# How the first attention of a hybrid decoder layer turns the probabilities of two query blocks: by TensorE, or by transposing transfers

## The chip, the core and the metric

The kernel runs on one core of a Trainium2 chip. The metric is the device time of one execution in microseconds (us). A core has TensorE (PE, whose weight loads are shown as PEld), VectorE (DVE), ScalarE (ACT), GpSimd (POOL) and SyncE (SP, which here issues DMA transfers); each works through its own queue of instructions in order, and they meet through semaphores.

## The reference

The reference is one decoder layer on 1024 tokens behind 16 learned meta tokens, D = 1024, in fp32. One projection feeds two groups of heads; their outputs are joined, projected and added to the residual, and a SwiGLU block follows. Cut to what matters here:

```python
def hybrid_mixer(u, pos, topk, w_in, ...):
    ...
    o_mla = causal_block_attention(q_mla, k_mla, v_mla)              # 8 heads, dense and causal
    ...
    o_dsa = indexed_sparse_attention(q_s, k_s, v_s, q_i, k_i, w_i, topk)   # 8 heads, selected keys
    o = jnp.concatenate([o_mla.reshape(...), o_dsa.reshape(...)], axis=-1)
    return o @ w_o

# inside both attentions, for each block of 128 queries
s = jnp.einsum('bqhd,bkhd->bhqk', qb, k) * scale
s = jnp.where(mask, s, -jnp.inf)
p = jax.nn.softmax(s, axis=-1)
o = jnp.einsum('bhqk,bkhd->bqhd', p, v)

h = h + hybrid_mixer(rmsnorm(h, ...), ...)
h = h + swiglu(rmsnorm(h, ...), w_gate, w_up, w_down)
return rmsnorm(h, final_norm_g)[:, N_META:t]
```

## The kernel before, in words

Queries are cut into eight blocks of 128. Attention is done in two passes: the **first attention** takes query blocks 0, 1 and 2 (`BLK_A`), the **second** blocks 3 to 7 (`BLK_B`). Each runs over 16 heads, first the eight latent ones (`mla_head`, half 0), then the eight sparse ones (`dsa_head`, half 1). Between and around them lie the first out-projection, the feed-forward block of the first 384 rows, the second out-projection and the feed-forward block of the rest. The matrix products of the attention scores and the feed-forward block are each made of two or three passes over a high and a low part of their operands.

The work is written as Python generators that are interleaved by hand, and the framework's scheduler then sets the order of the instructions in each engine's queue by a timeline of its own; an instruction that is later in the program can so stand earlier in a queue, if it is ready by that timeline. During the first heads of the first attention the rest of the latent projections (`mla_rest`, for rows 384 and up) is interleaved, and the first 12 tiles of the output weights are split into a high and a low part on GpSimd (`wo_load`, lines 995 and 996). The feed-forward block of the first rows fills TensorE during the second attention.

In each head and query block `b`, `scores` makes the scores by TensorE, adds the mask and finds the row's extreme in VectorE (line 785), and takes the exponential on ScalarE (line 792). Key blocks are 128 wide and there are `b + 2` of them. What is left is to turn the probabilities round, keys onto partitions, as a high and a low fp16 part, for the value product in `values` (lines 823 to 825: three matmuls for each key block). There are two ways to do that.

Where `b` is in `by_pe`, TensorE transposes the fp32 probabilities (line 799), ScalarE casts them out of PSUM to the high part (line 801) and VectorE makes the low part (line 802), both into tile `pE`. Otherwise, with a constant added to the extreme (line 790), the high part is cast in place of the rows into a buffer `hl` (line 812, VectorE), GpSimd subtracts it in pieces to give the low part (line 814), and SyncE issues one transfer that transposes both into tile `pT` (line 816):

```python
for c in cuts(n, 264):
    G.tensor_sub(pl_[:, c], pb[:, c], ph[:, c])
pT = pl.tile([P, 2 * (cfg["b1"] + 2), P], F16, name="pT", bufs=cfg["pT"])
nc.sync.dma_start_transpose(pT[:, 0:2 * nt], hl[:, 0:2 * nt * P])
```

The value products lag behind: finished probabilities wait in the list `todo`, and a block's values are taken when `depth` entries are in it. In the tables `CFG_A` and `CFG_B`, `hl`, `pT`, `pE`, `pb`, `pd`, `q`, `v` and `kn` are numbers of buffers. SyncE's queue also carries the loads of each sparse head: its keys and queries into `dkn` (two buffers) and `dkm` (one buffer), lines 917 and 923, its values into `vh` (two buffers), line 875, and the tiles of the output weights `wor` (line 991).

Of the kernel before, what the change touches and what calls it, by code (L numbers as in the profile page):

```python
# [43 lines left out]
BLK_A, BLK_B = tuple(range(NA)), tuple(range(NA, NB))  # L44
# [17 lines left out]

PREP_AT, PREP_N, WO_AT = 6, 2, 150
PH_ACT = BLK_B, ()
CFG_A = dict(depth=3, by_pe=set(BLK_A), order=list(BLK_A), pd=2, hl=2, pT=2, pb=3, pE=3, q=2, v=2, kn=2, ahead=0)
CFG_B = dict(depth=4, by_pe=set(), order=list(BLK_B), pd=2, hl=2, pT=2, pb=2, pE=2, q=2, v=2, kn=2, ahead=3)


# [30 lines left out]
def hybrid_layer(ctx, tc, a, out):  # L99
# [1046 lines left out]

    cfg = dict(CFG_A, s=ps_s, t=ps_t, o=ps_o, ck=(ckH, ckL), wk=(wkH, wkL), sel=selb, kT=kT_a, q_rows=q_a, v_rows=v_a)
    woa = ExitStack()
# [104 lines left out]
```

## Time and profile before

| what | value |
|---|---|
| time, median of 3 runs | 1523.28 us (1520.2 to 1530.37) |
| profiled execution: its own time | 1528.41 us |
| profiled execution: span of the instructions | 1526.6 us |
| TensorE busy | 1434.4 us, 94% of the span |
| VectorE busy | 907.2 us, 59% |
| ScalarE busy | 846.6 us, 55% |
| GpSimd busy | 796.2 us, 52% |
| share of the chain that ended last | PE 29%, of which lines 189 to 191 some 10% each |

Shares over the whole span are means over stages that have different limits. The first attention is the stretch from some 346 to 441 us, the second from 485 to 955 us. Busy times of single stretches and single instructions stand in the rows below; times in those rows count from the start of the span.

### The profile page before, as it was taken

Reading aid. Unit: us, or ns where it says so; the run is one execution under the profiler, and the core shown is the slowest. Engines: PE = TensorE matmul, PEld = TensorE weight load, DVE = VectorE, ACT = ScalarE, POOL = GpSimd, SP = SyncE. Lnnn points to the kernel's source line nnn. Section 1 sums busy time; section 2 is a strip of 40 time slices with the busy share of each in tenths; the row PEclk is TensorE's granted clock in tenths of the full one; section 3 lists DMA queues with packets and bytes.
Section 4 is the critical chain, followed back from the end, with each engine's and each line's share of the span. In section 5 each row is a group of like instructions: output and inputs, shape, how many; then the busy total and the mean of one; then the engine's idle time right before and its main releaser. Section 6 shows DMA issues by size and latency. Waiting matters only on the chain. (4 is left out here: it accounts for less than half of the span.)

```text
span 1526.6 us, 29766 instructions
## 1 busy us (share of the span) xinstructions
PE 1434.4 (94%) x10584; PEld 1332.2 (87%) x10584; DVE 907.2 (59%) x2447; ACT 846.6 (55%) x2038; POOL 796.2 (52%) x1121
## 2 busy tenths in 40 slices
PE   6999998999989899899899999999999999999997
PEld 5999998888778788788798899888899999999996
DVE  6879989948886876966866666415422222213225
ACT  5666678797889889797544453435412122122223
POOL 2663555212405678786887888531634344343342
PEclk9999999999999799999999999999999999999999
DMA  6123355224434787587799997431322222222221
GB/s 180 50 52 85 86 136 125 47 88 143 125 103 107 163 187 171 138 182 148 177 212 200 204 210 172 138 108 39 125 82 84 67 85 65 74 83 70 83 70 69
DMA packets 353732, 180.71 MB, mean 118 GB/s; under 512 B 196560, under 2 KB 341344, under 8 KB 353584
## 3 DMA queue, kind: packets, MB, share of 16 engines
q1 hardware_dynamic: 353584, 178.82, 46.7%
q8 instruction: 83, 1.36, 0.4%
q14 instruction: 65, 0.53, 0.1%
HBM read 120.77 MB, written 21.30 MB: 93 GB/s over the span
## 5 line engine op out<-in xcount | busy, mean ns | idle before, releaser
L184 POOL TENSOR_TENSOR wL<-raw,wH 128x256 fp32r<-128x256 f32 x528 | 399.1, 787 | 303.0 <-ACT wH L181 293.3
L181 ACT ACTIVATE wH<-raw 128x1024 fp32r<-128x1024 f32 x132 | 139.7, 1058 | 263.2 <-PE b L191 96.4
L189 PE MATMUL b<-ub,wH 128*128 128x384 f32 (+1 forms) x704 | 218.6, 311 | 1.2 <-ACT wH L181 1.2
L190 PE MATMUL b<-ub,wH 128*128 128x384 f32 (+1 forms) x704 | 218.5, 311 | 0.0
L191 PE MATMUL b<-ub,wL 128*128 128x384 f32 (+1 forms) x704 | 217.8, 310 | 0.0
L814 POOL TENSOR_TENSOR hl<-pd,hl 128x260 f16<-128x260 f32 (+5 forms) x256 | 168.4, 686 | 72.6 <-ACT hl L810 39.6
L189 PE MATMUL b<-wh,uH 128*128 128x256 f32 (+3 forms) x568 | 169.1, 298 | 5.3 <-DVE mlo L311 2.6
L191 PE MATMUL b<-wh,uL 128*128 128x256 f32 (+3 forms) x568 | 168.5, 297 | 0.0
L190 PE MATMUL b<-wl,uH 128*128 128x256 f32 (+3 forms) x568 | 168.1, 296 | 0.1
L1107 DVE TENSOR_TENSOR oh<-b,oh 128x512 f32<-128x512 f32 x146 | 99.2, 686 | 74.5 <-PE b L191 74.1
L189 PE MATMUL b<-wH,hH 128*128 128x512 f32 x352 | 140.5, 399 | 1.8 <-DVE oh L1107 0.8
L190 PE MATMUL b<-wL,hH 128*128 128x512 f32 x352 | 138.7, 394 | 0.0
L191 PE MATMUL b<-wH,hL 128*128 128x512 f32 x352 | 136.0, 393 | 0.4 <-DVE hL L186 0.4
L189 PEld LDWEIGHTS b<-ub,wH 128*128 128x128 f32 x704 | 132.8, 189 | 3.1 <-ACT wH L181 1.5
L190 PEld LDWEIGHTS b<-ub,wH 128*128 128x128 f32 x704 | 132.2, 188 | 1.2
L191 PEld LDWEIGHTS b<-ub,wL 128*128 128x128 f32 x704 | 132.1, 188 | 1.1
L189 PE MATMUL b<-ua,wH 128*128 128x384 f32 x352 | 122.0, 347 | 4.0 <-ACT wH L181 4.0
L375 ACT ACTIVATE js<-sc,bs 128x528 bf16<-128x528 int16 (+7 forms) x128 | 120.8, 944 | 4.1 <-DVE sc L430 1.7
L191 PE MATMUL b<-ua,wL 128*128 128x384 f32 x352 | 121.0, 344 | 0.0
L190 PE MATMUL b<-ua,wH 128*128 128x384 f32 x352 | 120.9, 343 | 0.0
L1093 DVE SCALAR_TENSOR_TENSOR sg<-sg,b 128x384 f32<-128x384 f32 x66 | 33.5, 508 | 144.5 <-ACT sg L1092 144.5
L189 PEld LDWEIGHTS b<-wh,uH 128*128 128x128 f32 x568 | 108.6, 191 | 7.4 <-DVE mlo L311 3.4
(326 smaller groups left out, 4026.6 us busy)
## 6 DMA issues: line engine op xcount, KB each, us to landing
raw<-in_w_gate SPq DMA_DIRECT2D x44, 512.0 KB, 4.1
raw<-in_w_up SPq DMA_DIRECT2D x44, 512.0 KB, 4.0
raw<-in_w_down SPq DMA_DIRECT2D x44, 512.0 KB, 3.6
wor<-in_w_o SPq DMA_DIRECT2D x64, 128.0 KB, 2.6
wraw<-in_w_in SPq DMA_DIRECT2D x40, 128.0 KB, 2.3
vh<-v_x SPq DMA_DIRECT2D x16, 288.0 KB, 3.8
xt<-in_x SPq DMA_DIRECT2D x8, 512.0 KB, 4.3
ks_x<-st SPq DMA_DIRECT2D x32, 128.0 KB, 2.2
```

The source lines that it names most:

```text
L181: S.activation(h, src, AF.Copy)
L184: G.tensor_sub(l[:, c], src[:, c], h[:, c])
L189: PE.matmul(o, lh, rh, start=first, stop=False)
L190: PE.matmul(o, lh, rl, start=False, stop=False)
L191: PE.matmul(o, ll, rh, start=False, stop=last)
L375: S.activation(act_junk()[:, :n_keys(b)], y[b], AF.Sign, bias=cols[0], accum_out=cnt)
L814: G.tensor_sub(pl_[:, c], pb[:, c], ph[:, c])
L1093: V.scalar_tensor_tensor(sg, sg, 1.0, pg, op0=OP.add, op1=OP.mult)
L1107: V.tensor_add(oh[t][:, cs], po, oh[t][:, cs])
```

## The change

The table of the first attention is altered in one line. Only block 0 stays with TensorE; the probabilities of blocks 1 and 2 take the other way, cast, subtracted and transposed by a transfer. `todo` becomes one entry deeper, there are three `hl` buffers and four `pT`, and the buffers of TensorE's way go from three to two.

```diff
 PREP_AT, PREP_N, WO_AT = 6, 2, 150
 PH_ACT = BLK_B, ()
-CFG_A = dict(depth=3, by_pe=set(BLK_A), order=list(BLK_A), pd=2, hl=2, pT=2, pb=3, pE=3, q=2, v=2, kn=2, ahead=0)
+CFG_A = dict(depth=4, by_pe={0}, order=list(BLK_A), pd=2, hl=3, pT=4, pb=2, pE=2, q=2, v=2, kn=2, ahead=0)
 CFG_B = dict(depth=4, by_pe=set(), order=list(BLK_B), pd=2, hl=2, pT=2, pb=2, pE=2, q=2, v=2, kn=2, ahead=3)
```

Since the scheduler sets the order anew, instructions of other lines move as well. Three places follow; a row gives the line, the operation, the tiles (out<-in), the size, and how often it stands there in a row.

GpSimd's queue in the later latent heads of the first attention: the difference between before (-) and after (+). `wor`, `woh` and `wol` are a raw tile of the output weights and its two parts.

```order
+L814 TENSOR_TENSOR hl_5318<-pd,hl_5318 128x136 x2
+L814 TENSOR_TENSOR hl_5319<-pd,hl_5319 128x200 x2
+L995 TENSOR_SCALAR woh<-wor 128x256 x2
+L996 TENSOR_TENSOR wol<-wor,woh 128x256
+L814 TENSOR_TENSOR hl_5320<-pd,hl_5320 128x136 x2
+L995 TENSOR_SCALAR woh<-wor 128x256 x2
+L996 TENSOR_TENSOR wol<-wor,woh 128x256
+L814 TENSOR_TENSOR hl_5318<-pd,hl_5318 128x200 x2
 L995 TENSOR_SCALAR woh<-wor 128x256
-L996 TENSOR_TENSOR wol<-wor,woh 128x256 x3
-L995 TENSOR_SCALAR woh<-wor 128x256 x3
```

The splits of the output weights stood by themselves; now the subtractions of blocks 1 and 2 stand between them.

SyncE's queue in the sparse heads of the first attention, before:

```order
L923 DMA dkm<-ks_m 16x128
L917 DMA dkn<-ks_x 128x3x128
L917 DMA dkn<-qs_x 128x3x128
L875 DMA vh<-v_x_94 128x2x256
L923 DMA dkm<-ks_m 16x128
```

The same place after:

```order
L816 DMA_TRANSPOSE pT<-hl_5320 128x8x128
L816 DMA_TRANSPOSE pT<-hl_5318 128x6x128
L917 DMA dkn<-ks_x 128x3x128
L923 DMA dkm<-ks_m 16x128
L875 DMA vh<-v_x_94 128x2x256
L917 DMA dkn<-qs_x 128x3x128
L816 DMA_TRANSPOSE pT<-hl_5319 128x8x128
L816 DMA_TRANSPOSE pT<-hl_5320 128x6x128
```

Two transposing transfers per head (six 128-column blocks for query block 1, eight for block 2) now stand in the one queue with the loads. The load of `vh` waits until the values that last used its buffer are done, as it did.

TensorE's queue where the second attention ends and the second out-projection begins, before. `ua`, `wH`, `hH` belong to the feed-forward block of the first rows, `oh` is the joined output of the heads, `ub` its transposed halves:

```order
L191 MATMUL b_15676<-ua,wL 128x384
L189 MATMUL b_15731<-wH,hH 128x512
L190 MATMUL b_15731<-wL,hH 128x512
L191 MATMUL b_15731<-wH,hL 128x512
L189 MATMUL b_15739<-wH,hH 128x512
L190 MATMUL b_15739<-wL,hH 128x512
L191 MATMUL b_15739<-wH,hL 128x512
L189 MATMUL b_12518<-woh,ub 128x256
```

The same place after:

```order
L825 MATMUL b_12347<-vh,pT 128x64
L1014 MATMUL b_12399<-ident,oh_5124 128x128 x4
L1014 MATMUL b_12406<-ident,oh_5125 128x128 x4
L1014 MATMUL b_12413<-ident,oh_5125 128x128 x4
L189 MATMUL b_12512<-woh,ub 128x256
L189 MATMUL b_12542<-woh,ub 128x256
```

Matmuls of the feed-forward block stood between the last values and the first products of the out-projection; now the first products follow the transposes directly.

## Rows read from the trace of the kernel before

**Rows 1.** Busy time of each engine, by stretch of the first attention; granted clock, DMA share.

```profile
346.00:372.00 26.00, 24.71 (x161) 21.41 (x160) 22.68 (x65) 18.86 (x53) 7.22 (x16) 0.93 0.34 106
372.00:380.00 8.00, 7.38 (x82) 6.61 (x81) 6.33 (x20) 6.67 (x22) 1.75 (x4) 1.00 0.80 259
380.00:400.00 20.00, 19.55 (x229) 17.11 (x227) 16.71 (x52) 18.21 (x65) 17.64 (x24) 1.00 0.50 147
400.00:436.00 36.00, 30.99 (x363) 26.40 (x362) 30.85 (x93) 29.38 (x103) 0.64 (x1) 1.00 0.37 102
```

**Rows 2.** ScalarE's timeline: block 0's exponential of heads 3, 8 and 15.

```profile
379.45 0.42 ACT L792 ACTIVATE pb<-pb,sm 128x144 f32<-128x144 f32 x1 [0.27 <-DVE sm L785]
...
402.11 0.41 ACT L792 ACTIVATE pb<-pb,sm 128x144 f32<-128x144 f32 x1 [0.38 <-DVE sm L785]
...
435.73 0.41 ACT L792 ACTIVATE pb<-pb,sm 128x144 f32<-128x144 f32 x1
```

**Rows 3.** Groups by line and shape, 405 to 440 us.

```profile
L799 PE MATMUL b<-ident,pb 128*128 128x128 f32 x67 | 11.5, 282 | 1.8 <-DVE pE L802 0.9 <-ACT pb L792 0.8
...
L802 DVE SCALAR_TENSOR_TENSOR pE<-b,pE 128x512 f16<-128x512 f32 x8 | 5.5, 685 | 0.9 <-ACT pE L801 0.9
...
L802 DVE SCALAR_TENSOR_TENSOR pE<-b,pE 128x384 f16<-128x384 f32 x8 | 4.4, 553 | 0.6 <-ACT pE L801 0.6
...
L801 ACT ACTIVATE pE<-b 128x384 f16<-128x384 f32 x7 | 3.5, 498 | 1.0 <-PE b L799 1.0
```

**Rows 4.** TensorE's timeline within one sparse head.

```profile
411.28 0.64 PE L799 MATMUL b<-ident,pb 128*128 128x128 f32 x4
411.76 0.19 PE L825 MATMUL b<-vh,pE 128*128 128x64 f16 x1
...
411.81 0.19 PE L824 MATMUL b<-vh,pE 128*128 128x64 f16 x1
```

**Rows 5.** GpSimd's groups by line and shape in the second attention.

```profile
L814 POOL TENSOR_TENSOR hl<-pd,hl 128x220 f16<-128x220 f32 x15 | 9.1, 608 | 0.0
...
L383 POOL TENSOR_TENSOR bs<-bs 128x1 f32<-128x1 f32 x4 | 0.8, 192 | 0.2
```

**Rows 6.** GpSimd's groups by line and shape, 375 to 402 us.

```profile
L995 POOL TENSOR_SCALAR woh<-wor 128x256 fp32r<-128x256 f32 x12 | 10.1, 850 | 7.1 <-PE b L825 6.3 <-DMA wor<-in_w_o 0.8
L996 POOL TENSOR_TENSOR wol<-wor,woh 128x256 fp32r<-128x256 f32 x12 | 8.5, 728 | 0.0
```

**Rows 7.** VectorE's groups by line and shape in the second attention.

```profile
L790 DVE TENSOR_SCALAR sm<-sm 128x1 f32<-128x1 f32 x77 | 11.3, 147 | 1.2
...
L812 DVE CAST hl<-pd 128x528 f16<-128x528 f32 x8 | 5.4, 680 | 6.4 <-ACT pd L792 3.1 <-ACT sg L1092 2.2 <-DMA pT<-hl 1.0
```

**Rows 8.** Everything on line 812, whole span: ns min/median/max.

```profile
L812 DVE CAST hl<-pd x40: 425/702/1237, 722.3 to 942.0; 128x528 f16<-128x528 f32 x8, 128x656 f16<-128x656 f32 x8, 128x784 f16<-128x784 f32 x8, 128x912 f16<-128x912 f32 x8
```

**Rows 9.** Everything on tile pT, whole span.

```profile
L816 SPq DMA_TRANSPOSE pT<-hl x80: 1259/2060/4361, 479.1 to 945.8; - x80
...
DMA to landing us min/median/max: 3.3/4.5/7.6
```

**Rows 10.** DMA issues, 405 to 435 us: median us to landing.

```profile
dkn<-ks_x SPq DMA_DIRECT2D x5, 192.0 KB, 2.4
...
vh<-v_x SPq DMA_DIRECT2D x6, 128.0 KB, 2.2
```

**Rows 11.** Everything on line 875, whole span.

```profile
L875 SPq DMA_DIRECT2D vh<-v_x x24: 332/430/1107, 335.3 to 905.3; - x24
```

**Rows 12.** Everything on tile pE, whole span.

```profile
L823 PE MATMUL b<-vh,pE x72: 189/193/203, 404.3 to 440.7; 128*128 128x64 f16 x72
```

**Rows 13.** Busy time by stretch, second attention and later.

```profile
485.00:955.00 470.00, 440.75 (x3725) 396.68 (x3724) 331.94 (x841) 315.86 (x675) 367.05 (x517) 0.97 0.81 178
955.00:965.00 10.00, 7.63 (x42) 6.38 (x41) 3.27 (x5) 3.69 (x6) 8.07 (x11) 1.00 0.60 156
```

**Rows 14.** TensorE's waits, 925 to 1075 us.

```profile
PE b L189 <- ACT woh L181: 4.3, 4, 2.9
```

## The prediction

> **What bounds the kernel now.** The shares over the span say TensorE, but the change acts in 95 of 1527 us, so I first cut the first attention into stretches [rows 1]; of the engine columns the order is TensorE, its weight loads, VectorE, ScalarE, GpSimd. From 346 to 372 us, with the latent projections beside the heads, TensorE is busy 24.71 of 26 us. From 380 to 400 it is busy 19.55 of 20, with GpSimd at 17.64 on the output weights. In the sparse heads, 400 to 436, no engine is full: TensorE 30.99 of 36, VectorE 30.85, ScalarE 29.38; a head there is a chain that passes from engine to engine. GpSimd and the transfers are idle in that stretch (0.64 us of 36; a DMA share of 0.37). The pace comes from ScalarE's timeline: block 0's exponential of heads 3, 8 and 15 starts at 379.45, 402.11 and 435.73 us [rows 2]. That makes (402.11 − 379.45)/5 = 4.53 us for a head from 3 to 8, and (435.73 − 402.11)/7 = 4.80 us for a sparse one. The last value product is at 440.7 us [rows 12]. Then, from 485 to 955 us, TensorE is busy 440.75 of 470 [rows 13].
>
> **What the change removes.** Seven of a head's nine transposes on TensorE (three for block 1, four for block 2). Four of them occupy it from 411.28 to 411.76 us [rows 4], 0.12 us each: 0.84 us per head, 13.4 us over 16 heads. VectorE loses its two low halves, 0.553 + 0.685 = 1.24 us per head; ScalarE its two casts, 0.5 us for the shorter one and no less for the longer, so 1.0 or more [rows 3].
>
> **What it adds.** VectorE casts 272 and 400 columns per head. The cast of 528 columns takes 680 ns and the shortest of all casts of that line 425 [rows 7, 8]; a small operation takes 147. By proportion to 680 the two make 0.35 + 0.52; if the fixed 147 counts, 0.42 + 0.55. With two additions at 0.147 that is 1.16 to 1.26 us (0.94 if the casts go at the faster rate of the 425 one). So VectorE gains 0 to 0.3 us per head out of some 4.1 busy (30.85 × 4.80 / 36). **TensorE and ScalarE are relieved, VectorE hardly**: the pace of a sparse head can't fall much below 4 us, and the most to be won there is 8 × (4.80 − 4.0) = 6 us.
>
> GpSimd subtracts two pieces of 136 and two of 200 columns. 220 columns take 608 ns and its smallest operation 192 [rows 5], which gives (608 − 192)/220 = 1.89 ns per column, 449 and 570 ns a piece, so 2 × 0.449 + 2 × 0.570 = **2.04 us per head**; straight by columns it is 1.86.
>
> SyncE issues 32 transposing transfers, each a new wait. None exists in the first attention; in the second, 80 of 10 to 18 blocks land in 3.3 us at least and 4.5 at the median [rows 9]. Ordinary loads of similar or smaller size in the sparse heads land in 2.4 and 2.2 [rows 10]. For six and eight blocks I take 3.2 us, next to the fastest of those of ten, with 2.4 and 4.5 as ends, since the DMA queues are half empty here.
>
> The Trainium skill, "VectorE: DVE Perf Modes", The three transpose paths, gives a 128×128 transpose as 390 ns on TensorE and 1309 ns on the DMA crossbar, and its Rules for kernel authors choose TensorE where the result may go to PSUM: that speaks against this change. By its figure 14 blocks a head are an estimated 18 us in series, four times the present pace. The rows differ on both sides: ten blocks land in 3.3 us [rows 9], TensorE needs 0.12 us [rows 4].
>
> **Stage by stage.** The sum stands against the profiled execution, 1528.41 us (span 1526.6 and some 2 around it), which is 5 above the median.
>
> (a) 346 to 372 us, TensorE full. Some two heads' transposes fall away there at 0.84 us: **−2** (0 to −3). GpSimd's subtractions join the rotary steps, but it is busy 7.22 of 26 us.
>
> (b) Heads 4 to 7, 380 to 400 us. Before, GpSimd does its 12 pairs of weight splits (10.1 + 8.5 = 18.6 us, [rows 6]) in one piece beside the heads, and no head waits for it. After, they stand between the subtractions of blocks 1 and 2, which the heads do wait for: 18.6 + 4 × 2.04 = 26.8 us of GpSimd in what took 4 × 4.53 = 18.1, or **+8.7** if all of it must pass in order. A deeper `todo` lets a part spill into the sparse heads, where GpSimd is idle. I take **+8** (0 if the backlog is swallowed, +9).
>
> (c) Sparse heads. In SyncE's queue the load of `vh` waits for the values two heads back, and the next transposes stand behind that load, as do `dkn` and `dkm`. This is a loop per head: block 2's and block 1's 21 value matmuls at 0.03 us [rows 4] 0.63, issue of the `vh` load and of one `dkn` load at 0.43 each [rows 11] 0.86, landing 3.2: 4.7 us, against the present 4.80. So **0**. With a landing of 2.4 the loop is 3.9 and VectorE's 4 us hold: −6. With 4.5 it is 6.0: 8 × 1.2 = +9.
>
> (d) Tail. Now the last head's chain (score, transposes on TensorE, values) ends 5.0 us after its exponential (440.7 − 435.73). After, block 2 of the last head goes through exponential 0.4, cast 0.55, subtractions 1.1, transfer 3.2 and values 0.4 to 0.7, some 6.2 after its reduction, which itself follows block 0's exponential by some 1.5 to 2, with nothing left to hide it: 7.7 to 8.2 instead of 5.0, so **+3** (+1 to +4).
>
> (e) Later stages. The matmuls of the feed-forward block before the first products of the second out-projection are used up earlier. TensorE waits there 4.3 us for the split output weights [rows 14], and from 955 to 965 us it is busy 7.63 of 10 [rows 13]. Without that cover up to +6 more; but matmuls moved earlier fill holes in the second attention, where 29 us are idle (470 − 440.75), as much as −6. Neither end is nearer to a row: **0**.
>
> TensorE's clock should not matter: it was granted 1.00 in a stretch with TensorE busy 7.63 of 10 us [rows 13], and the sparse heads after the change leave it about (30.99 − 7.5 × 0.84)/36 = 69%. If it does fall, the tail and its successors get longer.
>
> Sum: −2 + 8 + 0 + 3 + 0 = **+9** on 1528.4. Put to the median, 1523.3 + 9 = **1532 us**.
>
> **The rivals.** *Relief.* Transposes land like ordinary loads (2.4 us) and GpSimd's backlog is hidden by the depth: −2 + 0 − 6 + 3 = −5, or 1518; with (e) at −6, 1512. For it: idle transfers and idle GpSimd from 400 us on. Against: every transfer on tile `pT` took 3.3 us or more. The Trainium skill, "Advanced Engine Details and Errata", X-Bar Transpose (TRN2), says that transpose DMAs are as fast as regular ones. The transfers of the second attention alone don't bear that out here, though they carry more blocks.
>
> *Queue loop, the slow side.* Transposes land at the 4.5 us median. Then SyncE's loop, not an engine, sets the sparse heads at 6.0 us: +9 more on top of the +9, 1541, and with a tail longer by another 1.3 us, 1543. It decides as soon as the landing passes 3.3 us (4.80 − 1.49), and passes the 1% from a landing near 4. For it: the median row. Against: those transfers had 10 to 18 blocks and a busier DMA (0.81 against 0.37).
>
> *Cancelled.* GpSimd's splits slip into the sparse heads without a wait, (b) is +2 and relief and tail balance: −2 + 2 − 2 + 3 = +1, 1524.
>
> *The edit has no effect* can be left out: the instruction order shows the transfers and the missing transposes.
>
> **How the numbers follow.** Forecast 0.42, queue loop 0.28, cancelled 0.15, relief 0.15. One per cent, 15 us, is about what a measurement of this kernel tells from no change: faster is below 1508, slower above 1538.5. The forecast has 0.34 within 1% and 0.08 above; the queue loop 0.22 above and 0.06 within; cancelled is within; relief 0.11 within and 0.04 below. So faster 0.04, same 0.66, slower 0.30. The range takes in relief with its (b) and (c) gains halved for the low end, 1515, and for the high end the queue loop with a longer landing and half of (e), 1543 + 4 = 1547.
>
> **What would show it.** Right if, in the changed profile, heads 4 to 7 wait on GpSimd (line 814, behind 995 and 996) and take some 6.5 us each; if sparse heads keep about 4.8 us; if `pT` of six and eight blocks lands in 3 to 3.5 us; and if the last value product lies some 3 us further behind the last exponential. Wrong if a head takes 6 us with TensorE waiting on `pT` and SyncE on the values; or if GpSimd's backlog shows no wait in a head; or if the later stages, from 485 us on, are longer or shorter by more than 6 us, where I have only bounds.

## The result, and the profile after

The changed kernel is slower: 1569.47 us at the median of six runs (1561.59 to 1574.28), against 1523.74 for the kernel before, at the median of six runs too (the table ahead has three of them); the ratio is 1.0288 [1.026, 1.0317]. The prediction was 1532, with a range up to 1547. The profiled execution took 1570.14 us with a span of 1568.3, so 41.7 us more than the span before (1526.6).

The first view is the table by stretch, of the kernel after. As in [rows 1], the columns are TensorE, its weight loads, VectorE, ScalarE, GpSimd, the granted clock, the DMA share and GB/s.

```profile
346.00:372.00 26.00, 24.24 (x167) 21.12 (x168) 24.40 (x74) 18.69 (x54) 10.87 (x22) 0.87 0.52 136
381.00:425.00 44.00, 32.14 (x243) 26.60 (x241) 24.36 (x90) 20.03 (x68) 29.38 (x46) 0.58 0.71 158
425.00:457.00 32.00, 24.48 (x243) 19.62 (x244) 21.23 (x80) 19.71 (x70) 12.05 (x24) 0.83 0.79 155
457.00:473.00 16.00, 11.89 (x120) 10.53 (x119) 9.57 (x28) 6.86 (x23) 3.01 (x6) 0.79 0.45 91
```

From 381 to 425 us no engine is full: the fullest is TensorE with 32.14 of 44, and at a clock of 0.58 (1.00 before) its matmuls take longer (a value product from 392 to 420 us, at 0.50, 242 ns at the median; 193 before [rows 12]). ScalarE is idle for more than half the time. That is the picture of engines that wait for each other.

The second view is ScalarE's timeline with block 0's exponentials of heads 3, 8 and 15, after, as in [rows 2].

```profile
381.07 0.42 ACT L792 ACTIVATE pb<-pb,sm 128x144 f32<-128x144 f32 x1 [0.90 <-DVE sm L785]
...
416.81 0.42 ACT L792 ACTIVATE pb<-pb,sm 128x144 f32<-128x144 f32 x1 [0.84 <-DVE sm L785]
...
457.02 0.41 ACT L792 ACTIVATE pb<-pb,sm 128x144 f32<-128x144 f32 x1
```

Heads 3 to 8 take (416.81 − 381.07)/5 = 7.15 us each instead of 4.53, heads 8 to 15 (457.02 − 416.81)/7 = 5.74 instead of 4.80. The last value product of the first attention comes at 472.0 us instead of 440.7, which is 15.0 us behind the last exponential instead of 5.0. So the 31.3 us that this attention ends later are 1.6 at its start, 13.1 in heads 3 to 8, 6.6 in heads 8 to 15 and 10.0 in the tail. These are numbers of one execution: in the sixth and the tenth run below, whose first attention has the same order of instructions on all four compute engines, the last value comes at 464.3 and 464.4 us, and heads 3 to 9 take 41.0 us instead of 44.0.

That leaves 10.4 us that are lost behind the first attention, where no line was changed. They are found by following ScalarE and VectorE. Query blocks 5, 6 and 7 of the second attention need the list of kept keys; ScalarE finds it for blocks 6 and 7 by a chain of small steps (line 375), one block after the other, and VectorE turns it into a mask (lines 438 to 451). The next fence is the timeline of these two engines before, where the chain for block 7 ends.

```profile
737.07 1.16 ACT L375 ACTIVATE js<-sc,bs 128x1040 bf16<-128x1040 uint16 x1
...
757.42 0.28 DVE L451 TENSOR_TENSOR sc<-sc,cbias 128x128 bf16<-128x128 bf16 x1
757.62 0.51 DVE L785 CUSTOM_DVE_ANT_0 pd<-b,sc 128x348 f32<-128x348 f32 x1
```

And the same place after:

```profile
777.40 1.16 ACT L375 ACTIVATE js<-sc,bs 128x1040 bf16<-128x1040 uint16 x1
...
799.75 0.65 DVE L451 TENSOR_TENSOR sc<-sc,cbias 128x128 bf16<-128x128 bf16 x1
800.32 0.51 DVE L785 CUSTOM_DVE_ANT_0 pd<-b,sc 128x348 f32<-128x348 f32 x1
```

In both traces the reduction of the first sparse head over block 7 (line 785, which reads the mask as `sc`) starts at once when the mask is done: 757.42 and 757.62, 799.75 and 800.32. From the mask to the end of the span it is 769.2 us before and 768.6 after: on the clock, the whole loss is there by 800 us. The search starts 3.7 us (before) and 2.5 us (after) behind the last value product of the first attention, takes 293.8 and 304.0 us, and VectorE needs another 19.2 and 21.2 for the mask. The difference of the masks is 31.3 − 1.2 + 10.2 + 2.0 = 42.3 us, against 41.7 in the span.

TensorE's account reads differently. Here is its busy time from the last value product of the first attention to the mask, on to the last value of the second attention, and on to the end, before:

```profile
440.70:757.40 316.70, 290.81 (x2392) 262.75 (x2388) 235.34 (x612) 260.52 (x592) 217.73 (x306) 0.96 0.71 158
757.40:952.80 195.40, 189.82 (x1666) 172.55 (x1667) 129.02 (x342) 92.41 (x186) 165.78 (x235) 1.00 0.90 198
952.80:1526.60 573.80, 552.92 (x3404) 518.71 (x3403) 180.76 (x359) 167.01 (x309) 229.44 (x311) 0.99 0.27 83
```

And after:

```profile
472.00:799.80 327.80, 306.70 (x2490) 279.35 (x2485) 245.13 (x614) 268.60 (x600) 229.46 (x324) 0.97 0.70 160
799.80:1008.80 209.00, 187.39 (x1609) 165.03 (x1608) 128.37 (x341) 89.42 (x183) 162.70 (x233) 0.97 0.89 187
1008.80:1568.30 559.50, 538.93 (x3329) 507.44 (x3328) 173.14 (x349) 161.18 (x302) 217.57 (x295) 0.98 0.27 81
```

Behind the first attention TensorE is busy for the same 1033 us in both, and for 1028 to 1039 us in all 17 traces, with 50 to 63 us idle. That is enough to pass the 31.3 us on to the end, with the search or without it. Only the other 10.4 us are idle time added behind the first attention, and it is not added ahead of the mask (25.9 us idle before, 21.1 after) but between the mask and the last value of the second attention (5.6 and 21.6): TensorE did 16 us more of its work while the mask was awaited, and lacked it afterwards.

### The profile page after: what moved, and what is told of

Its sections match the earlier page's. It is cut to its first block, busy times and chain, and to the rows that moved or that the text cites. A ratio compares the mean times of both kernels' runs of the same rounds, so it can differ in the third digit from the quotient of the medians.

```text
span 1568.3 us, 29685 instructions
## 1 busy us (share of the span) xinstructions
PE 1447.7 (92%) x10472; PEld 1340.0 (85%) x10472; DVE 911.5 (58%) x2487; ACT 838.6 (53%) x2006; POOL 826.0 (53%) x1185
## 4 chain that ended last, share of the span: by engine, by line
PE 44%; DVE 13%; DMA 10%; POOL 9%; ACT 7%; issue 7%; SPq 0%; DVEq 0%; POOLq 0%; ACTq 0%
PE b L189 13%; PE b L191 13%; PE b L190 13%; POOL wL L184 4%; DMA pT<-hl 4%; POOL hl L814 3%; PE b L783 2%; DMA wor<-in_w_o 2%; DMA raw<-in_w_up 2%; DVE jk L390 2%; ACT js L375 2%; DMA raw<-in_w_gate 1%; DVE pd L785 1%; DVE oh L1107 1%; ACT pd L792 1%
## 5 line engine op out<-in xcount | busy, mean ns | idle before, releaser
L814 POOL TENSOR_TENSOR hl<-pd,hl 128x228 f16<-128x228 f32 (+7 forms) x320 | 197.5, 644 | 128.0 <-DVE hl L812 72.1
L792 ACT ACTIVATE pd<-pd,sm 128x272 f32<-128x272 f32 (+5 forms) x112 | 93.9, 839 | 57.7 <-DVE sm L790 52.3
```

The costliest lines, as they stand in the source:

```text
L792: S.activation(pb, pb, AF.Exp, bias=mn, scale=-1.0, accum_out=z)
```

## The experiments

The table has what the expectations speak of, from the trace of each run: head 3 to 9 and head 9 to 15 by block 0's exponentials, the last value product of the first attention, the search on ScalarE, the mask of block 7, and the rest from the mask to the end of the span; us throughout.

| run | ratio to before, interval | 3 to 9 | 9 to 15 | last value | search, its length | mask | mask to end |
|---|---|---|---|---|---|---|---|
| before | | 28.5 | 27.8 | 440.7 | 444.4 to 738.2, 293.8 | 757.4 | 769.2 |
| after | 1.0288 [1.026, 1.0317] | 44.0 | 31.9 | 472.0 | 474.6 to 778.6, 304.0 | 799.7 | 768.6 |
| 1 block 1 only | 0.9988 [0.9961, 1.0016] | 27.3 | 27.8 | 443.0 | 446.2 to 734.0, 287.8 | 757.6 | 767.5 |
| 2 block 2 only | 1.005 [1.0028, 1.0072] | 28.0 | 29.6 | 451.9 | 454.1 to 756.0, 301.9 | 773.0 | 761.0 |
| 3 depth 4 alone | 1.0044 [1.0021, 1.0067] | 27.8 | 25.5 | 438.0 | 441.7 to 747.3, 305.6 | 763.7 | 765.5 |
| 4 TensorE kept busy | 1.025 [1.0209, 1.0291] | 36.4 | 44.2 | 473.4 | 475.5 to 780.0, 304.5 | 803.7 | 760.9 |
| 5 splits held back | 1.0187 [1.016, 1.0214] | 30.0 | 37.3 | 456.7 | 458.7 to 759.4, 300.7 | 775.3 | 778.8 |
| 6 filler held back | 1.0267 [1.0237, 1.0297] | 41.0 | 31.9 | 464.3 | 466.8 to 779.4, 312.6 | 800.6 | 765.5 |
| 7 weights on ScalarE's queue | 1.025 [1.0223, 1.0277] | 48.2 | 34.2 | 472.8 | 475.0 to 784.8, 309.8 | 805.4 | 759.1 |
| 8 more buffers for loads | 1.0205 [1.0176, 1.0235] | 40.8 | 33.6 | 469.1 | 471.3 to 773.4, 302.1 | 792.4 | 765.3 |
| 9 before, two chains | 1.0042 [1.0017, 1.0066] | 28.3 | 27.9 | 440.1 | 443.7 to 710.0, 266.2 | 754.9 | 779.8 |
| 10 after, two chains | 1.0195 [1.0143, 1.0247] | 41.0 | 31.9 | 464.4 | 466.9 to 747.1, 280.2 | 786.3 | 764.8 |
| 11 block 1 only, again | one run | 27.9 | 28.2 | 444.8 | 448.0 to 736.1, 288.1 | 758.1 | 768.3 |
| 12 block 1, two chains | 1.0061 [1.0037, 1.0085] | 27.7 | 27.1 | 442.5 | 445.7 to 714.3, 268.6 | 756.3 | 772.6 |
| 13 splits held, two chains | 1.014 [1.0112, 1.0168] | 31.6 | 35.9 | 457.8 | 459.9 to 724.8, 264.9 | 766.0 | 775.9 |
| 14 splits held to head 11 | 1.0214 [1.0182, 1.0247] | 32.8 | 36.9 | 465.8 | 467.4 to 775.9, 308.5 | 796.1 | 766.2 |
| 15 deeper | 1.0171 [1.0146, 1.0197] | 31.3 | 37.0 | 459.0 | 461.0 to 728.5, 267.5 | 768.4 | 782.7 |

The scheduler sets every order anew for an edited kernel, so a run also carries changes of order that its edit doesn't name; so a single run alone shows no cause below some 10 us (the third run, where only the depth and its buffers differ, is some 7 us from the kernel before, and two executions of one order end the first attention 7.7 us apart).

**One block by transfers, block 1 or block 2.** The first two runs divide the change.

```diff
-CFG_A = dict(depth=4, by_pe={0}, ..., hl=3, pT=4, pb=2, pE=2, ...)
+CFG_A = dict(depth=4, by_pe={0, 2}, ..., hl=2, pT=2, pb=2, pE=3, ...)
```

> Only block 1 goes by transfers (16 of six blocks; GpSimd subtracts 2 x 0.45 us a head); block 2 stays on TensorE; depth 4, two hl, two pT, three pE. Theory Q (queues: the splits of the output weights, the subtractions, the loads and the transposing transfers wait for each other in turn on GpSimd's and SyncE's queues, and TensorE's clock only follows): half the waits go, the first attention's last value comes at some 455 us (before 440.7, after 472.0), TensorE's clock in 390 to 430 us is above 0.8. Theory C (clock: one stall of TensorE lets its clock fall to a half, and that makes the heads slow): the stall before 390 us is still there, last value at 465 or later. Theory F (filler: how many feed-forward matmuls are left behind the last value product of the second attention decides the second half; 76 before, 0 after): 80 are left here, so from the last value of the first to that of the second attention 512 us as before (after: 537), and the whole by Q and F is 1540 us.

1521.77 us, the same as before. Block 1 alone costs 2.3 us in the first attention, less than any theory gave. The splits stand among its subtractions here too, from 385 to 415 us, and heads 3 to 9 take 27.3 us, no longer than before (28.5).

```diff
-CFG_A = dict(depth=4, by_pe={0}, ..., hl=3, pT=4, pb=2, pE=2, ...)
+CFG_A = dict(depth=4, by_pe={0, 1}, ..., hl=2, pT=2, pb=2, pE=4, ...)
```

> Only block 2 goes by transfers (16 of eight blocks; GpSimd subtracts 2 x 0.57 us a head); block 1 stays on TensorE; depth 4, two hl, two pT, four pE. Q: last value of the first attention at 455 to 460 us. C: 465 or later. F: 6 feed-forward matmuls are left behind the second attention, so its last heads lie bare as in the changed kernel, TensorE has 8 us or more idle in the last 30 us before its last value, and the whole is 1550 to 1558 us; without F it would be 1540.

1532.41 us. Block 2 alone costs 11.2 us in the first attention, 5.5 of them in the tail (10.5 instead of 5.0), 4.4 ahead of head 3, none in heads 3 to 9, although the splits stand among the subtractions from 390 to 420 us. Q and F gave more (455 us or later, 1540 us or more). Together the two blocks cost 31.3, so **the parts don't add up**: 2.3 + 11.2 = 13.5, against 31.3, or 23.6 by the sixth and tenth runs.

**The depth alone.**

```diff
-CFG_A = dict(depth=3, by_pe=set(BLK_A), ..., pb=3, pE=3, ...)
+CFG_A = dict(depth=4, by_pe=set(BLK_A), ..., pb=3, pE=4, ...)
```

> All three blocks on TensorE as before, only the depth goes from 3 to 4 (with four pE). No transfer is added. The first attention ends within 3 us of 440.7 by Q and C alike. F: 30 feed-forward matmuls are left behind the second attention instead of 76, so a part of the cover is gone: 3 to 8 us slower than before, 1527 to 1532. If the filler's place means nothing: 1524 within 3.

1531.39 us, as F expected, but the table suggests another reason: the first attention ends 2.7 us earlier and the search is 11.8 us longer (305.6), so the mask comes 6.3 us later.

**TensorE kept busy.**

```diff
         S.activation(pb, pb, AF.Exp, bias=mn, scale=-1.0, accum_out=z)
+        if b in (1, 2):
+            for g0 in range(0, nt, 4):
+                pt = cfg["t"]()
+                for j in range(g0, min(nt, g0 + 4)):
+                    c1 = min(n, (j + 1) * P)
+                    PE.transpose(pt[0:c1 - j * P, (j - g0) * P:(j - g0 + 1) * P], pb[:, j * P:c1], ident)
```

> The changed kernel with the seven transposes of each head put back on TensorE as dead work: nobody reads what they write. The transfers stay and carry the values. C: TensorE is busier by 0.12 us for each of 112 transposes and its clock holds 0.9 or more from 390 to 430 us, heads there take some 5.5 us, last value of the first attention at 455 to 460 us, the whole 1555. Q: heads 4 to 9 still take 7 us or more whatever the clock, last value at 470 to 478 us, the whole 1568 to 1578. F: none of the feed-forward matmuls is left behind the second attention, so its end lies bare in either case.

1564.55 us. The first fence is the stretch from 390 to 430 us of the changed kernel, the second of this run, the third of the sixth run, whose first attention has the order of the changed kernel on every engine.

```profile
390.00:430.00 40.00, 31.33 (x229) 26.19 (x230) 21.82 (x76) 17.93 (x61) 29.74 (x46) 0.51 0.68 152
```

```profile
390.00:430.00 40.00, 29.82 (x272) 24.49 (x270) 22.90 (x79) 18.41 (x64) 29.72 (x46) 0.78 0.63 153
```

```profile
390.00:430.00 40.00, 27.88 (x250) 23.20 (x250) 25.57 (x88) 18.94 (x66) 27.56 (x45) 0.71 0.77 155
```

The clock is 0.78 instead of 0.51, though not the 0.9 that C asked for, and the last value comes at 473.4 us, as before the edit and as Q had it (the whole, 1568 or more by Q, came lower). Here heads 3 to 9 are quicker (36.4) and heads 9 to 15 slower (44.2), which is an order that also moved. The sixth run compares better: same order, 0.71 instead of 0.51, and from head 3 to the last value 86.3 us instead of 90.9, so up to 4.6 us go with that step of the clock. What a clock of 1.00 throughout would give back no run shows. In the changed kernel from 440 to 460 us it is nearly that:

```profile
440.00:460.00 20.00, 14.56 (x167) 11.35 (x165) 13.83 (x55) 13.32 (x47) 8.38 (x18) 0.93 0.76 149
```

Heads 12 to 15 still take 5.15 us each there, against 4.24 before. So the clock alone is not the cause.

**The weight splits held back.**

```diff
                 raw = wo.tile([P, cw], F32, name="wor", bufs=4)
+                if on_pool:
+                    V.tensor_copy(raw[0:1, 0:1], zs[0:1, 2, 1, 7:8])
```

> The changed kernel, but the loads of the first 12 tiles of the output weights wait (by a small write into their tile) for the last sparse head's sum of block 2, so their splits on GpSimd can't stand among the subtractions. Theory S (splits and subtractions in one queue, with the splits' loads in SyncE's queue between the transposing transfers, are what slows heads 4 to 9): from head 3's to head 9's exponential 28 to 33 us (before 28.4, changed kernel 44.0). Theory L (SyncE's loop of transposing transfers and the sparse heads' own loads slows them): 40 us or more, as the splits are not in that loop. The splits, 18.6 us of GpSimd, must now fall behind the heads: the first value of the second attention comes up to 12 us later than heads alone would give. Theory F (feed-forward matmuls used up before the end of the second attention cost 10 us or more there): 80 are left behind the second attention here, so from its first value to the end 1041 us as before (changed kernel: 1055). By S and F the whole is 1535 to 1545; by L 1555 or more.

1555.09 us. Heads 3 to 9 are back at 30.0 us: S holds for them, and L falls. The edit takes both away, the splits from GpSimd's queue and their loads from SyncE's. The whole, though, is at the 1555 that L gave. The groups of GpSimd in the changed kernel from 381 to 425 us show what is gone (columns: busy us, mean ns, idle before and what ended it):

```profile
L995 POOL TENSOR_SCALAR woh<-wor 128x256 fp32r<-128x256 f32 x12 | 10.5, 879 | 8.8 <-DMA wor<-in_w_o 5.0 <-issue 3.7
L996 POOL TENSOR_TENSOR wol<-wor,woh 128x256 fp32r<-128x256 f32 x12 | 9.0, 758 | 0.0
L814 POOL TENSOR_TENSOR hl<-pd,hl 128x200 f16<-128x200 f32 x10 | 5.4, 560 | 1.7 <-DVE sm L790 1.7
L814 POOL TENSOR_TENSOR hl<-pd,hl 128x136 f16<-128x136 f32 x12 | 5.2, 450 | 3.4 <-DVE hl L812 3.4
```

GpSimd is busy for 30.1 us there and idle for 13.9: 8.8 ahead of a split and 5.1 ahead of a subtraction. Each kind waits for its own source with the other kind queued behind it. The chain of waits of the changed kernel from 384 to 430 us runs through these up to some 408 us, and through transposing transfers and loads of keys behind that (start, us, what):

```profile
387.11 3.75 DMA wor<-in_w_o
390.86 0.07 issue
390.93 0.87 POOL woh L995
391.80 0.06 POOL wol L996
391.86 0.59 issue
392.45 0.97 POOL hl L814 x2
393.43 1.63 POOL woh L995 x2
...
402.27 2.99 DMA wor<-in_w_o
...
407.69 4.65 DMA pT<-hl
```

But with the splits away heads 9 to 15 take 37.3 us, more than in the changed kernel, and the whole gains 14 us where S and F gave 24 or more. The second attention now starts at 486.9 us, 1.3 later than before, and yet 26 us are lost after it, although 80 feed-forward matmuls are left behind it: F's 1041 us are missed. Much of this is the first value that came early, beside the splits and the first out-projection: counted from the last value of the first attention, 16.0 us are lost ahead of it and 11.5 behind it.

**The filler held back.**

```diff
                 raw = fw.tile([P, D], F32, name="raw", bufs=2)
+                if f == NF - 1 and len(blocks) == NA and name == "w_gate":
+                    V.tensor_copy(raw[0:1, 0:1], zs[0:1, 5, 1, 7:8])
```

> The changed kernel, but the gate weights of the first rows' last feed-forward slice wait for the last sparse head's sum of block 5, so the last 84 of the feed-forward matmuls can run only in the last 25 us of the second attention or behind it. The first attention is left as in the changed kernel (last value at 470 to 474 us). F: the matmuls then fill the holes that lay bare at the end (11 us of TensorE's 29 idle from 980 to 1009), and from the first value of the second attention to the end it takes 1041 to 1047 us instead of 1055; the whole 1556 to 1561. If the filler's place means nothing: 1055 and 1569.

1567.99 us. The first value of the second attention came at 505.1 us and the span ended at 1566.1, which are 1061 us, not the 1041 to 1047 of F. From 980 us to the last value at 1005 TensorE is still idle for 5.6 of 25 us, so the end of the second attention is filled in part, and that gives nothing. From here on the theory is T: the search.

**The weights on another queue, and more buffers.**

```diff
-                ld(raw, a["w_o"][0, d * P:(d + 1) * P, c * cw:(c + 1) * cw])
+                (nc.scalar.dma_start if on_pool else ld)(raw, a["w_o"][0, d * P:(d + 1) * P, c * cw:(c + 1) * cw])
```

> The changed kernel, but the output weights' first 12 tiles are loaded by ScalarE's queue instead of SyncE's, so no transposing transfer stands behind a weight load that waits for GpSimd. The splits still stand among the subtractions on GpSimd. If the tie between the two queues (SyncE waits for GpSimd's splits, GpSimd for SyncE's loads) is the cost, head 3 to head 9 takes 30 to 36 us; if GpSimd's order alone is the cost, 40 us or more. 0 feed-forward matmuls are left behind the second attention, so its end lies bare; the whole 1555 to 1560 in the first case, 1565 to 1570 in the second.

1564.45 us, heads 3 to 9 at 48.2. By the expectation that means GpSimd's order alone, and GpSimd does wait no less than in the changed kernel (11.8 us ahead of splits, 6.8 ahead of subtractions from 377 to 425 us). But the edit also moved something else. The transposing transfers from 380 to 425 us, in the changed kernel and then in this run:

```profile
DMA to landing us min/median/max: 2.7/3.2/4.8
```

```profile
DMA to landing us min/median/max: 2.7/4.2/7.7
```

Of the chain of waits from 377 to 425 us of this run 52% is transfers into `pT`. So whether the splits do harm by GpSimd's order or by their loads is not separated.

```diff
-CFG_A = dict(..., q=2, v=2, kn=2, ahead=0)
+CFG_A = dict(..., q=2, v=3, kn=3, ahead=0)
-WO_NA, WO_NB, WO_P = ND + 4, ND, ND + 4
+WO_NA, WO_NB, WO_P = ND + 2, ND, ND + 2
-            km = pl.tile([NM, 2, HD], F32, name="dkm", bufs=1)
+            km = pl.tile([NM, 2, HD], F32, name="dkm", bufs=2)
```

> The changed kernel with a third buffer for the sparse heads' keys, queries and values and a second one for the meta keys (ten instead of 12 split tiles of the output weights make room), so SyncE's queue waits less for TensorE. L: heads 4 to 9 get 1.5 us or more faster each (head 3 to head 9 at 35 us or less), and the sparse heads from 9 to 15 take 29 us instead of 31.9. S: head 3 to head 9 stays at 40 to 45 us. 6 feed-forward matmuls are left behind the second attention. The whole 1556 by L, 1566 to 1572 by S.

1557.63 us. The heads don't follow L (40.8 and 33.6 us, not 35 or less and 29); the total came near L's all the same, with two splits fewer, a first attention that ends 2.9 us earlier and a mask that comes 7.3 us earlier. Heads 3 to 9 at 40.8 are no gain over the 41.0 of the sixth and tenth runs, which have two buffers.

**Two search chains.** The searches of blocks 6 and 7 run side by side.

```diff
-TOPK_B = [([[5]], False, 2), ([[6], [7]], True, 3)]
+TOPK_B = [([[5]], False, 2), ([[6]], True, 2), ([[7]], True, 2)]
```

> The kernel before, but in the second attention the searches of the kept keys of query blocks 6 and 7 on ScalarE run as two chains side by side instead of one after the other. Theory T (the search chain on ScalarE starts when the first attention ends, takes some 294 us, ends at 738 us, and the sparse heads of the second attention wait for it; the feed-forward matmuls that TensorE does meanwhile are missing at the end): the search ends before 680 us, the pause before the first sparse head (44.5 us from the eighth latent head's first exponential to the next) shrinks to 35 us or less, and the whole is 1510 to 1522. If the search gates nothing: 1523 within 5, or slower by ScalarE's crowding.

1531.35 us, 0.4% slower than before: not T's 1510 to 1522, but the other case, crowding on ScalarE. The search ends 28 us sooner, but the latent heads beside it are slowed: the eighth latent head's exponential of block 3 comes at 748.5 us instead of 719.8. In VectorE's timeline of this run the sparse head no longer starts with the mask:

```profile
754.91 0.25 DVE L451 TENSOR_TENSOR sc<-sc,cbias 128x128 bf16<-128x128 bf16 x1
765.50 0.50 DVE L785 CUSTOM_DVE_ANT_0 pd<-b,sc 128x348 f32<-128x348 f32 x1
```

> The changed kernel with the same two search chains side by side. The first attention ends at some 470 us as in the changed kernel. T: the search no longer ends at 779 us but before 720, the sparse heads of the second attention start without the 56 us pause, and the 10 to 15 us that the second attention and what follows lost come back: from its first value to the end 1041 to 1046 us instead of 1055, the whole 1553 to 1560. If the search gates nothing: 1569 within 5.

1554.34 us, 15 less than the changed kernel, and from the first value of the second attention to the end 1040.3. Of the span's 17.2 us less than in the changed kernel, 7.6 come from a first attention that ended at 464.4 us (the same order there); 9.6 are left for what follows, 5.5 of them less idle time of TensorE. The mask is 13.4 us sooner, and the sparse head again follows it at once:

```profile
786.32 0.64 DVE L451 TENSOR_TENSOR sc<-sc,cbias 128x128 bf16<-128x128 bf16 x1
786.99 0.52 DVE L785 CUSTOM_DVE_ANT_0 pd<-b,sc 128x348 f32<-128x348 f32 x1
```

The eleventh run, in spite of its label, is the kernel of the first once more, with one chain, at 1528.2 us in a single run:

> The kernel with transfers for block 1 alone once more, as the partner of the kernel with two chains: 1517 to 1528.

> Transfers for block 1 alone (the first attention as quick as before, last value at 443 us) with the two search chains side by side. T: what the chain costs comes back on top, 1508 to 1520; if the search gates nothing, 1522 within 5.

The edits of the first and the ninth run together: 1533.7 us, no gain, as in the ninth run. Where the first attention ends in time, the search chain is not the only limit.

**Both cures.** The edits of the fifth and the tenth run together:

> Splits held back as in the fifth run, and two search chains side by side as in the tenth. S and T together: heads 3 to 9 take 28 to 33 us (S), the first value of the second attention comes at 485 to 492 us, and the sparse half of the second attention no longer starts at 790 us but before 775 (T), so from its first value to the end 1040 to 1050 us instead of 1067, and the whole 1528 to 1542. If T is wrong: 1067 and 1555.

1547.26 us. Heads 3 to 9 take 31.6, the first value of the second attention comes at 494.3, and 1047.6 us follow. The two edits give back 22 of the 45.7 us; the forecast of 1528 to 1542 was too low, so S and T together are not the whole cause.

**Splits held to head 11, and a longer lag.** The first is the fifth run with `zs[0:1, 2, 1, 3:4]` as the place to wait for.

> As in the fifth run, but the loads of the weight tiles wait only for sparse head 11, so the splits come among the last four heads' subtractions. S: heads 3 to 9 at 28 to 33 us as with the longer hold, and the splits' cost shows up later: from head 9 to head 15 38 us or more (changed kernel 31.9), last value of the first attention at 458 to 468 us, the whole 1550 to 1562. If the place of the splits doesn't matter in the sparse heads: 9 to 15 at 32 to 37 us and 1545 or less.

1558.11 us; heads 3 to 9 at 32.8, heads 9 to 15 at 36.9. The edit did not bring the splits where it was meant to: the first starts at 448.9 us, the others behind head 15's exponential (450.9 us), up to 475.9. So heads 9 to 15 are without splits here as in the fifth run (37.3; splits from 453 us on), and both runs say that the splits are not what makes the sparse heads slow. What splits among the subtractions of the sparse heads would cost stays untried. Here they stand in the tail, which takes 14.9 us instead of the fifth run's 11.6; the search took 308.5 us.

```diff
-CFG_A = dict(depth=4, by_pe={0}, ..., hl=3, pT=4, ...)
+CFG_A = dict(depth=5, by_pe={0}, ..., hl=4, pT=5, ...)
-WO_NA, WO_NB, WO_P = ND + 4, ND, ND + 4
+WO_NA, WO_NB, WO_P = ND + 2, ND, ND + 2
```

> As the thirteenth run (splits held back, two search chains), with depth 5, four hl and five pT; ten instead of 12 split tiles make room. If the sparse heads of the first attention are slow (6.0 us each in the thirteenth run, 4.63 before) because a transposed block comes back too late for the lag that the buffers allow (VectorE waits 4.4 us for hl and TensorE 4 to 6 us for pT between 405 and 445 us), a longer lag gives head 9 to head 15 in 28 to 32 us instead of 35.9 and the whole 1538 to 1543, the tail being longer by a block. If SyncE's order of transfers and loads sets them: 34 to 38 us and 1545 to 1552.

1551.89 us, heads 9 to 15 at 37.0: a longer lag doesn't help, and both numbers lie where the expectation put them if SyncE's order of transfers and loads sets these heads. That order itself was changed in no run.

## Why the prediction was wrong

The sign was right and the size was not: +9 was forecast, +41.7 came in the profiled execution. Of the signs that were to show the forecast right, two came (heads 3 to 8 at 7.15 us with waits on GpSimd, a landing of 3.2 us) and two did not: the sparse heads take 5.74 us instead of some 4.8, and the last value lies 10.0 us further behind the last exponential instead of some 3. Of the signs of being wrong, that of the later stages came: from the first value of the second attention to the end it is 1055.4 us instead of 1041.0, more than 6 us longer.

**(a), and what was priced.** The durations held. Subtractions of 136 and 200 columns take 450 and 560 ns (449 and 570 were worked out). The transfers of six and eight blocks land as taken, 3.2 us; this is everything on `pT` from 350 to 475 us, after:

```profile
L816 SPq DMA_TRANSPOSE pT<-hl x32: 1210/1232/1337, 354.6 to 466.0; - x32
...
DMA to landing us min/median/max: 2.7/3.2/5.0
```

The rule of the Trainium skill that was weighed there ("VectorE: DVE Perf Modes", Rules for kernel authors: TensorE for a 128×128 transpose whose result may go to PSUM) agrees with the result for both blocks together, but not with block 1 alone, which costs nothing by transfers (0.9988), and not by its price of 1309 ns: eight blocks land in some 3 us.

Term (a) itself was −2 and came out at +1.6. The relief is there: head 2's exponential starts at 367.19 us, 4.8 earlier than before (371.98). Between head 2 and head 3 6.4 us are lost again; why is not shown, but the fifth run loses them too (363.94 to 377.83 us), so it is not the splits.

**(b), the step that failed first.** "26.8 us of GpSimd in what took 4 × 4.53 = 18.1, or +8.7 if all of it must pass in order" took GpSimd's work as a sum without idle time. An upper bound of +9 holds only if its queue never waits. It waits for 13.9 us between 381 and 425, while splits and subtractions stand alternately and each kind waits for another source. Heads 3 to 8 lost 13.1 us, and heads 3 to 9 lost 15.5. That it takes the splits is shown by the fifth and fourteenth runs (30.0 and 32.8 us with the splits away). That it takes both blocks is shown by the first and second (27.3 and 28.0 us with the splits among the subtractions of one block). That it is GpSimd's order and not the splits' loads in SyncE's queue is argued from its waits and not shown, as the seventh run delayed the transfers too.

**(c) was mis-sized** at 0, inside its range of −6 to +9: heads 8 to 15 lost 6.6 us, 5.74 us a head against the 4.7 of the loop. It is not the number of buffers for the loads (eighth run), not the splits (fifth) and not the lag (fifteenth). From head 9 to head 15 one block by transfers costs at most 1.8 us and two cost 4.1, or 8.1 to 9.5 with the splits held back. Two of the loop's terms were too small. The landing is 3.3 us at the median from 425 to 457 us, but 3.6 in the mean, with four of twelve over 4 us. And the time for which SyncE's queue is held by issuing a transposing transfer, 1.23 us, was put at nothing; the two of a head go one behind the other, as SyncE's timeline after shows:

```profile
435.27 2.56 SPq L816 DMA_TRANSPOSE pT<-hl  x2
437.93 0.52 SPq L917 DMA_DIRECT2D dkn<-ks_x  x1
440.14 0.36 SPq L875 DMA_DIRECT2D vh<-v_x  x1
440.56 0.46 SPq L923 DMA_DIRECT2D dkm<-ks_m  x1
441.11 2.58 SPq L816 DMA_TRANSPOSE pT<-hl  x2
443.78 0.53 SPq L917 DMA_DIRECT2D dkn<-qs_x  x1
```

SyncE issues for 23.3 of the 32 us. With the second transfer 1.23 us behind the first the loop is an estimated 5.9 us, near the 5.74; the fifteenth run fits that. No run changed this order, so it is argued and the cause stays open.

**(d) was mis-sized**: the tail is 15.0 us instead of the 7.7 to 8.2 worked out. The last transfer leaves at 466.0 us, 9 us behind the last head's first exponential, and lands 3.05 us later; TensorE does matmuls of the first out-projection from 466.9 us on, and the last values come behind them at 472. The tail of the second run (10.5 with block 2 alone) shows block 2's part. The working itself was short: its terms from the exponential on add up to 5.7 to 6.0 us, where 6.2 was written.

**TensorE's clock** was said not to matter, from a stretch at 1.00 with TensorE 76% busy. It fell to 0.50 from 392 to 420 us, after a stretch with TensorE busy 7.82 of 12 us (380 to 392) in which it waited for a transfer; once fallen, it stayed there though TensorE was 22.30 of the 28 us busy. The row was no evidence: it was one short stretch. The step between 0.51 and 0.71 is worth up to 4.6 us (sixth run), and the clock alone is not the cause (fourth run, and heads 12 to 15).

**(e), the step that failed second.** The price of "later stages" was put at 0, and sought at the end of the second attention, in feed-forward matmuls that are used up. What came is 10.4 us behind the last value of the first attention. Two things are needed to read them. First, a delay of the first attention is passed on in full: TensorE has 1033 us of work behind it in both kernels, and its idle time there did not shrink to take up the 31 us (52.4 us before, 63.3 after). Second, there is a chain that can add to it: last value, search on ScalarE, mask, first sparse head over block 7. In all 17 traces the search starts 1.6 to 3.7 us behind the last value product; why it doesn't start earlier was not tried. In the ten traces with one search chain and unmoved splits the span ends 759 to 769 us behind the mask; counted from the last value it is 1082 to 1102 us, so the mask is the better predictor of the end there. Over all 17 it is not (759 to 783 and 1082 to 1102). While the sparse heads wait for a later mask, TensorE works off feed-forward matmuls that it then lacks; holding some of them back gave nothing (sixth run).

That the longer search (by 10.2 us) is the cause of the 10.4 us is argued and not shown. Its length differs between 288 and 313 us among kernels with one chain, whose search is the same code; where the scheduler puts the steps in ScalarE's queue would explain it, which is argued too. The tenth run supports the chain (mask 13.4 us sooner, 9.6 us less behind the first attention), and the ninth and twelfth limit it: with the first attention in time, a search that ends some 20 to 28 us sooner makes the kernel no faster; in the ninth run the latent heads beside it are slowed.

**The rivals.** The queue loop, the rival on the slow side, had the right sign. Its condition, a landing above 3.3 us, was not met at the median (3.2), and yet the sparse heads came near its 6.0 us; it is not refuted for them, and it has nothing on heads 3 to 8, where most was lost. Relief and cancellation are refuted. The low end of the range, 1515, does not come out of its own words (relief with halved gains in (b) and (c) is 1525, or 1519 with (e) at −6); the miss lies at the other end.

No version beats the kernel before: block 1 alone by transfers is equal to it (0.9988 [0.9961, 1.0016]).

## What to carry to other kernels

When an edit puts work of a latency chain into a queue that has its own work, the sum of the durations is not an upper bound of its price: the waits of two alternating sources come on top. Here 30.1 us of work on GpSimd took 44 us with both blocks, while the same mixture with one block cost its heads nothing. In a queue that issues transfers, the time for which each issue holds it belongs in the sum. Before a delay in one stage is called local, look at how full the fullest engine is in all that follows (TensorE's 1033 us came out the same), and at what starts when that stage ends and runs as a serial chain on another engine (a search of some 300 us on ScalarE). And halves of a change are worth timing apart: block 1 alone was free and block 2 alone cost 0.5%, where both cost 2.9%.

## What the runs showed of the hardware

TensorE's granted clock stayed at 0.50, its lower level of 1.2 GHz, for a long stretch with TensorE busy most of the time; these rows by stretch are of the changed kernel, the stall ahead of it first:

```profile
380.00:392.00 12.00, 7.82 (x66) 6.37 (x66) 7.12 (x29) 6.19 (x24) 3.87 (x7) 0.84 0.92 222
385.00:390.00 5.00, 1.54 (x12) 0.92 (x10) 2.99 (x12) 1.88 (x7) 1.11 (x3) 0.82 1.02 187
390.00:428.00 38.00, 29.71 (x216) 25.06 (x217) 19.93 (x69) 16.97 (x57) 28.24 (x44) 0.50 0.68 150
```

With the same order of instructions in the first attention of the sixth run the mean from 390 to 430 us was 0.71, so how long it stays low differs between executions. A transposing transfer of six or eight blocks occupies SyncE for 1.2 us and lands in 3.2 us at the median and 2.7 at the quickest; the ordinary loads of the sparse heads around it, from 425 to 457 us after, land in 2.1 to 2.8 at the median. With the DMA engines full (a share of 1.02 from 385 to 390 us) one took 4.75.
